# Lead tiles of the FFN opening on normalized quarters: root spreads at fixed places, two lead tiles at a time

## The chip, the cores and the metric

The kernel runs on one core of one Trainium2 chip, in one launch. The metric is the device time of that launch in microseconds; the kernel before was timed three times (median 1522.23), and one further execution was recorded by the hardware profiler. TensorE multiplies matrices, VectorE and ScalarE work on 128-partition tiles, GpSimd does small copies here, and the DMA queues bring the weights in.

## The reference

One inference step of a two-layer decoder trunk with 1024 channels, for 512 prompt positions and 8 sequences of 8 sample positions (576 columns together). Layer 0 has a convolution and windowed attention as its mixer, layer 1 a Mamba-2 mixer; both mixers end in an output projection that is added to the residual `x`, and behind each stands the block that the change touches:

```python
def rmsnorm(x, g):
    xf = x.astype(jnp.float32)
    xf = xf * lax.rsqrt(jnp.mean(xf * xf, axis=-1, keepdims=True) + EPS)
    return xf.astype(x.dtype) * g
...
def conv_ffn(h, hist, w_gate, w_up, conv_w, conv_b, w_down):
    gate = h @ w_gate
    padded = jnp.concatenate([hist, gate], axis=1)
    gc = causal_dwconv(padded, conv_w, conv_b)
    y = (jax.nn.silu(gc) * (h @ w_up)) @ w_down
    return y, padded[:, -(FFN_CONV_WIDTH - 1):]
```

Here `h` is `rmsnorm` of the layer's residual with the norm's gains, `w_gate` and `w_up` have 2816 columns, and the convolution over time has width 3. All values are float32.

## The kernel before

**Products.** Activations lie with channels on the partitions: eight tiles `x0` to `x7` of 128 channels by 576 columns, worked on in two halves of 288 (`HALF`). A float32 product is three TensorE matmuls: each operand is split in a rounded high part and the residual low part, and high times high, high times low and low times high are added up in one PSUM bank (`mm3`, L286, L289, L290). For every tile of weights, ScalarE therefore makes `wh` (L276) and VectorE `wl` (L277), from a buffer `wr` that a DMA fills; `wr`, `wh` and `wl` have three buffers each.

**The norm.** The output projection (`out_proj`, L453) adds its tiles to `x` (`add_x`, L451), the last four for half 0 and then for half 1, and ScalarE and VectorE sum the squares (`sq_add`, L337). When a half is complete, `rstd` (L310) sums over the partitions on TensorE (`pt`, L317), takes the root on ScalarE (L324) and the reciprocal on VectorE (L325 to L329, which end in `dg`), and spreads the result over all partitions by a matmul (`pr`, L333), copied out as `rs` (L335).

**The opening of the FFN.** 22 tiles of gate and of up follow (`ffn`, L475). The first four of gate and two of up are lead tiles: plain products with a pair `h` = g*x, not yet normalized, made by `norm_tile` (high part L411 on ScalarE, low part L412 on VectorE) while the projection still runs. Their results are multiplied by `rs` when they leave PSUM: gate at L521, L524 and L525 on VectorE, up through the gate's SiLU at L510. Behind a gate tile, `gate_done` saves conv history (GpSimd, L497, L498) and computes conv (ScalarE L501, VectorE L503 twice) and SiLU (L506, L507); `gate_open` (L489, L490) begins a gate buffer on GpSimd.

All other tiles go in pairs through a Strassen scheme, seven products in place of eight (`Strassen`, L53 to L150; first product L106, L109, L110). It takes normalized activations in quarters (channels 0 to 511 or 512 to 1023, by half): B11, B12, B21, B22 and the sums T1 to T4. `combine` (L364) makes them between the lead tiles: `hf` = x*g*rs (L373), the differences (L376), and for each piece a high part (ScalarE L361) and a low part (VectorE L362). Its three stages run ahead of gate 3, up 0 and up 1. B12 is not a quarter of its own there. For a Strassen job the sums of weights `st` are made by VectorE (L66, L69 to L71), and their splits at L75 and L76.

**What sets the order.** Each engine runs its instructions in a fixed order that a scheduler derives from the program; an instruction that is marked (`keep_in_program_order`, or `pin=True` in `mm3`) keeps its place among TensorE's. Engines meet through semaphores, and a buffer with a new name waits for the readers of the old one.

## Time and profile before

| | |
|---|---|
| runs | 1522.0, 1522.23, 1522.6 us (median 1522.23) |
| profiled execution | 1524.2 us, of which the span of the instructions is 1522.4 |
| busy, share of the span | TensorE 97%, VectorE 79%, ScalarE 54%, GpSimd 13% |
| mean granted TensorE clock | 0.987 |
| opening of layer 0 | about 214 to 279 us |
| opening of layer 1 | about 1109 to 1173 us |

An opening is counted here from the matmuls `pt` of half 0 to the first product of the second Strassen job. In the profile a row of the timeline has the start, the duration, the engine and line, the operation, and "output <- inputs"; square brackets give idle time before it and what ended it. "PE" is TensorE, "PEld" its weight loads, "DVE" VectorE, "ACT" ScalarE, "POOL" GpSimd and "SPq" a DMA queue. A group row has the number of instructions, the total and mean (ns) duration, and the idle time ahead of them.

### The profile page before, as it was taken

Reading aid. Unit: us, or ns where it says so; the run is one execution under the profiler, and the core shown is the slowest. Engines: PE = TensorE matmul, PEld = TensorE weight load, DVE = VectorE, ACT = ScalarE, POOL = GpSimd, SP = SyncE. Lnnn points to the kernel's source line nnn. Section 1 sums busy time; section 2 is a strip of 40 time slices with the busy share of each in tenths; the row PEclk is TensorE's granted clock in tenths of the full one; section 3 lists DMA queues with packets and bytes.
Section 4 is the critical chain, followed back from the end, with each engine's and each line's share of the span. In section 5 each row is a group of like instructions: output and inputs, shape, how many; then the busy total and the mean of one; then the engine's idle time right before and its main releaser. Section 6 shows DMA issues by size and latency. Waiting matters only on the chain.

```text
span 1522.4 us, 28606 instructions
## 1 busy us (share of the span) xinstructions
PE 1470.3 (97%) x11179; PEld 1398.1 (92%) x11179; DVE 1207.7 (79%) x2283; ACT 827.2 (54%) x1650; POOL 191.2 (13%) x365
## 2 busy tenths in 40 slices
PE   8999997999999999999999999999897999999999
PEld 7968797999999999898988988998897999999998
DVE  7968899977787786778887787777899887877773
ACT  6357466644545443587755754656565554545441
POOL 0035103000000000011312102102002000000000
PEclk9999998999999999999999999999998999999999
DMA  7514221422223322236246245245213322233222
GB/s 225 157 37 115 83 97 29 138 84 84 84 85 99 108 80 64 72 101 208 70 141 196 72 129 178 83 132 167 80 56 97 98 84 84 85 105 99 88 69 84
DMA packets 74551, 157.81 MB, mean 104 GB/s; under 512 B 20383, under 2 KB 25119, under 8 KB 74415
## 3 DMA queue, kind: packets, MB, share of 16 engines
q1 hardware_dynamic: 74414, 155.97, 33.0%
q8 instruction: 88, 1.44, 0.4%
q14 instruction: 49, 0.39, 0.1%
HBM read 140.73 MB, written 15.21 MB: 102 GB/s over the span
## 4 chain that ended last, share of the span: by engine, by line
PE 40%; DVE 6%; ACT 2%; DMA 2%; issue 1%; SPq 0%; ACTq 0%
PE mm L290 8%; PE mm L286 8%; PE mm L289 8%; PE x L106 3%; PE x L109 3%; PE x L110 3%; DMA acb<-acd 2%; PE y L110 1%; PE y L106 1%; PE y L109 1%; DVE wl L277 1%; PE pst L1379 1%; PE z L109 1%; PE z L106 1%; PE z L110 1%; ACT wh L276 1%
## 5 line engine op out<-in xcount | busy, mean ns | idle before, releaser
L290 PE MATMUL mm<-hh,wl 128*128 128x288 f32 x1056 | 318.0, 303 | 22.0 <-DVE wl L277 22.0
L286 PE MATMUL mm<-hh,wh 128*128 128x288 f32 x1056 | 322.1, 306 | 7.4 <-ACT wh L276 5.2
L289 PE MATMUL mm<-hl,wh 128*128 128x288 f32 x1056 | 319.1, 303 | 0.7 <-DVE hl L309 0.4
L290 PEld LDWEIGHTS mm<-hh,wl 128*128 128x128 f32 x1056 | 203.7, 193 | 26.1 <-DVE wl L277 23.2
L286 PEld LDWEIGHTS mm<-hh,wh 128*128 128x128 f32 x1056 | 203.6, 193 | 16.2 <-ACT wh L276 5.6
L289 PEld LDWEIGHTS mm<-hl,wh 128*128 128x128 f32 x1056 | 203.6, 193 | 4.2 <-issue 1.6
L276 ACT ACTIVATE wh<-wr 128x1024 fp32r<-128x1024 f32 (+2 forms) x107 | 108.5, 1014 | 107.0 <-PE mm L289 88.9
L451 DVE TENSOR_TENSOR x<-x,mm 128x288 f32<-128x288 f32 x256 | 113.6, 449 | 51.8 <-PE mm L290 51.5
L277 DVE TENSOR_TENSOR wl<-wr,wh 128x1024 fp32r<-128x1024 f32 (+2 forms) x107 | 127.5, 1194 | 31.7 <-ACT wh L276 31.6
L290 PE MATMUL mm<-yh,vl 128*128 128x288 f32 x512 | 151.2, 295 | 0.0
L286 PE MATMUL mm<-yh,vh 128*128 128x288 f32 x512 | 151.1, 295 | 0.0
L289 PE MATMUL mm<-yl,vh 128*128 128x288 f32 x512 | 151.1, 295 | 0.0
L290 PE MATMUL mm<-yh,wl 128*128 128x288 f32 x448 | 133.9, 300 | 4.3 <-DVE wl L277 4.3
L286 PE MATMUL mm<-yh,wh 128*128 128x288 f32 x448 | 135.2, 303 | 0.0
L289 PE MATMUL mm<-yl,wh 128*128 128x288 f32 x448 | 134.6, 301 | 0.0
L75 ACT ACTIVATE wh<-st 128x512 fp32r<-128x512 f32 x152 | 92.1, 624 | 31.2 <-PE x L109 23.1
L76 DVE TENSOR_TENSOR wl<-st,wh 128x512 fp32r<-128x512 f32 x152 | 103.3, 686 | 2.1 <-ACT wh L75 0.7
L286 PEld LDWEIGHTS mm<-yh,vh 128*128 128x128 f32 x512 | 96.4, 188 | 0.0
L290 PEld LDWEIGHTS mm<-yh,vl 128*128 128x128 f32 x512 | 96.4, 188 | 0.0
L289 PEld LDWEIGHTS mm<-yl,vh 128*128 128x128 f32 x512 | 96.3, 188 | 0.0
L503 DVE SCALAR_TENSOR_TENSOR gconv<-gbuf,par,gconv 128x592 f32<-128x592 f32 x88 | 72.9, 831 | 25.1 <-ACT gconv L501 24.8
L290 PEld LDWEIGHTS mm<-yh,wl 128*128 128x128 f32 x448 | 85.3, 191 | 5.8 <-DVE wl L277 4.5
(395 smaller groups left out, 4001.2 us busy)
## 6 DMA issues: line engine op xcount, KB each, us to landing
wr<-in_w_gate SPq DMA_DIRECT2D x44, 512.0 KB, 3.6
wr<-in_w_up SPq DMA_DIRECT2D x44, 512.0 KB, 4.2
wr<-in_w_in_o SPq DMA_DIRECT2D x40, 512.0 KB, 3.6
wr<-in_w_down SPq DMA_DIRECT2D x64, 256.0 KB, 2.9
h<-in_h SPq DMA_DIRECT2D x32, 256.0 KB, 3.8
acb<-acd SPq DMA_DIRECT2D x32, 256.0 KB, 4.2
out_ssm_s<-h SPq DMA_DIRECT2D x32, 256.0 KB, 2.9
wr<-in_w_out_o SPq DMA_DIRECT2D x16, 512.0 KB, 3.8
```

The lines of the kernel that those rows point to most:

```text
L75: nc.scalar.activation(hi, src, AF.Copy)
L76: nc.vector.tensor_tensor(lo, src, hi.bitcast(F32), op=SUB)
L106: m = nc.tensor.matmul(out, hi[:, ws], xh, start=first and k == 0, stop=False, skip_group_check=skip)
L109: nc.tensor.matmul(out, hi[:, ws], xl, start=False, stop=False, skip_group_check=skip)
L110: nc.tensor.matmul(out, lo[:, ws], xh, start=False, stop=k == 3, skip_group_check=skip)
L276: nc.scalar.activation(hi[:, a:b], raw[:, a:b], AF.Copy)
L277: nc.vector.tensor_tensor(lo[:, a:b], raw[:, a:b], hi[:, a:b].bitcast(F32), op=SUB)
L286: first = nc.tensor.matmul(out, hi[:, ws], xh[:, sl], start=i == 0, stop=False)
L289: nc.tensor.matmul(out, hi[:, ws], xl[:, sl], start=False, stop=False)
L290: nc.tensor.matmul(out, lo[:, ws], xh[:, sl], start=False, stop=i == n - 1)
L451: nc.vector.tensor_tensor(self.x[m][:, sl], self.x[m][:, sl], p[:, :HB], op=ADD)
L503: nc.vector.scalar_tensor_tensor(cv[:, :592], g[:, k:592 + k], w(k), cv[:, :592], op0=MUL, op1=ADD)
```

## The change

The lead tiles take the normalized quarters too, so there is no pair `h`, no L411 or L412, and results leave PSUM by plain copies on ScalarE (gate) or as they did (up); `sl*rs` (L510) is gone. `rstd` is cut in two: `rstd_begin` (to `dg`) and `rstd_end` (spread and copy). At the last tile of the projection, the weights of gate 0 and 1 are loaded ahead of half 0, and gate 2 ahead of half 1; between them the root of half 0 is spread and `scaled(0)` makes B11 and B21, and the projection's last twelve matmuls are marked to keep their place. `lead` takes two gate tiles at a time and goes through the eight quarter pieces, six matmuls each: gates 0 and 1 on half 0, then gates 2 and 3, in whose middle half 1's root is spread and `scaled(1)` makes B12 and B22. Then come T1, gates 0 and 1 on half 1, T2, gates 2 and 3 on half 1, and up 0 and up 1. T3 and T4 are made behind the first Strassen job's `alpha`. B12 is one quarter more, and gate 1's weights are split as two tiles of 512 columns.

```diff
     def norm_begin(self, gname, early, quarters=None):
+        self.gname, self.early, self.ahead = gname, early, quarters
+        self.h = [] if quarters else [self.pair("h") for _ in range(8)]
...
+    def quarter(self, name, make):
+        src = [make(0)]
+        for k in range(4):
+            if k < 3:
+                src.append(make(k + 1))
+            nc.scalar.activation(q[k][:, 0:HB], src[k], AF.Copy)
+            nc.vector.tensor_tensor(q[k][:, HB:T], src[k], q[k][:, 0:HB].bitcast(F32), op=SUB)
+
+    def scaled(self, half):
+        for name, k0 in (("B11", 0), ("B21", 4)) if half == 0 else (("B12", 0), ("B22", 4)):
+            def make(k):
...
+                self.nc.vector.scalar_tensor_tensor(t, self.x[k0 + k][:, sl], self.pv(self.gname, k0 + k), self.rs[:, sl], op0=MUL, op1=MUL)
+                return t
+            self.quarter(name, make)
...
+            lead = norm and self.ahead and m == 7
+            if lead and hf == 0:
+                self.lead = [self.whole(self.ahead[0]), self.halved(self.ahead[1])]
+            if lead and hf == 1:
+                self.lead.append(self.whole(self.ahead[2]))
+                self.rstd_end(self.rs, root, HALF[0])
+                self.scaled(0)
...
+                if lead and hf == 0:
+                    root = self.rstd_begin(self.ssq, self.o1024, HALF[0])
...
-            if f < LEAD_U:
-                nc.vector.tensor_tensor(sl, sl, rs, op=MUL)
...
-                    nc.vector.tensor_tensor(gate_open(f)[:, 2:290], p[:, :HB], rs[:, :HB], op=MUL)
+                    nc.scalar.activation(gate_open(f)[:, 2:290], p[:, :HB], AF.Copy)
...
-                nc.vector.tensor_tensor(g[:, 290:514], p[:, 0:224], rs[:, HB:NP], op=MUL)
-                nc.vector.tensor_tensor(samples(g)[:, :, 2:10], bt(p[:, 224:288]), bt(rs[:, NP:]), op=MUL)
+                nc.scalar.activation(g[:, 290:514], p[:, 0:224], AF.Copy)
+                nc.scalar.activation(samples(g)[:, :, 2:10], bt(p[:, 224:288]), AF.Copy)
...
+        def lead(half, todo, mid=None):
+            names = ("B11", "B21") if half == 0 else ("B12", "B22")
+            banks = [self.pm() for _ in todo]
+            for k in range(8):
+                if mid and k == 4:
+                    mid()
+                t = self.hq[names[k // 4]][k % 4]
+                xh, xl = t[:, 0:HB], t[:, HB:T]
+                for bank, (ws, _) in zip(banks, todo):
+                    out = bank[:, :HB]
+                    hi, lo = [w[:, k % 4 * P:k % 4 * P + P] for w in ws[k // 4]]
+                    m = nc.tensor.matmul(out, hi, xh, start=k == 0, stop=False)
+                    if k in (0, 4):
+                        self.tc.keep_in_program_order(m)
+                    nc.tensor.matmul(out, hi, xl, start=False, stop=False)
+                    nc.tensor.matmul(out, lo, xh, start=False, stop=k == 7)
+            for bank, (_, evac) in zip(banks, todo):
+                evac(half, bank)
...
-        self.units([lead_gate(f) for f in range(3)], 3)
+        g01 = [(w, lead_gate(f)) for f, w in enumerate(self.lead[:2])]
+        lead(0, g01)
+        g23 = [(self.lead[2], lead_gate(2)), (self.whole(d["w_gate"][l, 3]), lead_gate(3))]
+        root = self.rstd_begin(self.ssq, self.o1024, HALF[1])
+        def other():
+            self.rstd_end(self.rs, root, HALF[1])
+            self.free(self.ssq)
+            self.scaled(1)
+        lead(0, g23, other)
         sums = self.combine()
         next(sums)
-        self.units([lead_gate(3)], 1)
+        lead(1, g01)
         next(sums)
-        self.units([lead_up(0)], 1)
-        next(sums)
-        self.units([lead_up(1)], 1)
-        self.free(self.rs, self.h)
+        lead(1, g23[:1])
+        u = [(self.whole(d["w_up"][l, 0]), lead_up(0))]
+        lead(1, g23[1:])
+        lead(0, u)
+        lead(1, u)
+        u = [(self.whole(d["w_up"][l, 1]), lead_up(1))]
+        lead(0, u)
+        lead(1, u)
```

In the engines' orders the change shows at three places. The first is VectorE at the end of layer 0's output projection, around the root of half 0 (`rv` and `dg`; `hl` is the low part of `h`, `wl` a lead tile's residual weights). Before:

```order
L451 TENSOR_TENSOR x4_81<-x4_81,mm_2606 128x288
L451 TENSOR_TENSOR x5_82<-x5_82,mm_2625 128x288
L325 RECIPROCAL rv_2596<-rv_2596 128x72
L412 SCALAR_TENSOR_TENSOR hl_2335<-x4_81,par_72,hh_2334 128x288
L327 TENSOR_SCALAR rv_2596<-rv_2596,rsc_74 128x72
L344 TENSOR_TENSOR ssq_2324<-ssq_2324,sq_2622 128x288
L328 SCALAR_TENSOR_TENSOR rv_2596<-dg_2595,rsc_74,rv_2596 128x72
L412 SCALAR_TENSOR_TENSOR hl_2337<-x5_82,par_72,hh_2336 128x288
L329 TENSOR_TENSOR dg_2595<-rv_2596,rsc_74 128x288
L344 TENSOR_TENSOR ssq_2324<-ssq_2324,sq_2641 128x288
```

and now, where `wl_2633` belongs to gate 2:

```order
L475 TENSOR_TENSOR x4_81<-x4_81,mm_2579 128x288
L475 TENSOR_TENSOR x5_82<-x5_82,mm_2596 128x288
L346 RECIPROCAL rv_2572<-rv_2572 128x72
L371 TENSOR_TENSOR ssq_2324<-ssq_2324,sq_2593 128x288
L348 TENSOR_SCALAR rv_2572<-rv_2572,rsc_74 128x72
L277 TENSOR_TENSOR wl_2633<-wr_2630,wh_2632 128x1024
L349 SCALAR_TENSOR_TENSOR rv_2572<-dg_2571,rsc_74,rv_2572 128x72
L371 TENSOR_TENSOR ssq_2324<-ssq_2324,sq_2610 128x288
L350 TENSOR_TENSOR dg_2571<-rv_2572,rsc_74 128x288
L475 TENSOR_TENSOR x6_83<-x6_83,mm_2613 128x288
L403 SCALAR_TENSOR_TENSOR hf_2643<-x0_77,par_72,rs_2325 128x288
```

The `hl` rows are gone, a `wl` has come between the steps of the root, and the first scaled piece stands two rows behind `dg`.

The second place is VectorE where the second half's scaled pieces begin in layer 0. Before, they were spread between the sums and the evacuations of the gate tiles:

```order
L373 SCALAR_TENSOR_TENSOR hf_2922<-x0_77,par_72,rs_2325 128x288
L373 SCALAR_TENSOR_TENSOR hf_2923<-x1_78,par_72,rs_2325 128x288
L376 TENSOR_TENSOR hf_2922<-hf_2922 128x288
L376 TENSOR_TENSOR hf_2923<-hf_2923 128x288
L373 SCALAR_TENSOR_TENSOR hf_2924<-x2_79,par_72,rs_2325 128x288
L524 TENSOR_TENSOR gbuf_2750<-mm_2812,rs_2325 128x224
L525 TENSOR_TENSOR gbuf_2750<-mm_2812,rs_2325 128x8x8
L376 TENSOR_TENSOR hf_2924<-hf_2924 128x288
```

Now two operations on the first Strassen job's weights (`wr_3181`) stand ahead of them:

```order
L349 SCALAR_TENSOR_TENSOR rv_2775<-dg_2774,rsc_74,rv_2775 128x72
L350 TENSOR_TENSOR dg_2774<-rv_2775,rsc_74 128x288
L66 TENSOR_TENSOR st0_3185<-wr_3181 128x512
L76 TENSOR_TENSOR dl_3191<-wr_3181,dh_3190 128x512
L403 SCALAR_TENSOR_TENSOR hf_2643<-x0_77,par_72,rs_2325 128x288
L403 SCALAR_TENSOR_TENSOR hf_2645<-x1_78,par_72,rs_2325 128x288
L403 SCALAR_TENSOR_TENSOR hf_2649<-x2_79,par_72,rs_2325 128x288
L392 TENSOR_TENSOR hqB12_2811<-hf_2643,hqB12_2811 128x288
```

All eight scaled pieces of the half follow in one run, and no evacuation stands between them.

The third place is VectorE ahead of the weights of up 0 in layer 0. Before, `wl_3072` closed a run of B22's pieces:

```order
L373 SCALAR_TENSOR_TENSOR hf_2928<-x6_83,par_72,rs_2325 128x288
L373 SCALAR_TENSOR_TENSOR hf_2929<-x7_84,par_72,rs_2325 128x288
L362 TENSOR_TENSOR hqB22_3057<-hf_2926,hqB22_3057 128x288
L362 TENSOR_TENSOR hqB22_3058<-hf_2927,hqB22_3058 128x288
L362 TENSOR_TENSOR hqB22_3059<-hf_2928,hqB22_3059 128x288
L362 TENSOR_TENSOR hqB22_3060<-hf_2929,hqB22_3060 128x288
L277 TENSOR_TENSOR wl_3072<-wr_3069,wh_3071 128x1024
```

and now `wl_3022` stands at the end of the sums and of two convolutions:

```order
L535 SCALAR_TENSOR_TENSOR gconv_2945<-gbuf_2755,par_72,gconv_2945 128x592
L392 TENSOR_TENSOR hqT2_2967<-hf_2663,hqT2_2967 128x288
L535 SCALAR_TENSOR_TENSOR gconv_2945<-gbuf_2755,par_72,gconv_2945 128x592
L535 SCALAR_TENSOR_TENSOR gconv_2956<-gbuf_2759,par_72,gconv_2956 128x592
L414 TENSOR_TENSOR hf_2669<-hf_2669,hf_2649 128x288
L535 SCALAR_TENSOR_TENSOR gconv_2956<-gbuf_2759,par_72,gconv_2956 128x592
L392 TENSOR_TENSOR hqT2_2968<-hf_2665,hqT2_2968 128x288
L414 TENSOR_TENSOR hf_2673<-hf_2673,hf_2653 128x288
L277 TENSOR_TENSOR wl_3022<-wr_3019,wh_3021 128x1024
```

Both pieces of T2 that are left, and all of T3 and T4, come behind it.

## The prediction

> **What bounds the kernel now.** I read three views: the page for the whole, TensorE's waits by releaser for where it stops, and the timeline and the table of windows for the places around those stops.

> ```profile
> span 1522.4 us, 28606 instructions
> PE 1470.3 (97%) x11179; PEld 1398.1 (92%) x11179; DVE 1207.7 (79%) x2283; ACT 827.2 (54%) x1650; POOL 191.2 (13%) x365
> PE mm L290 <- DVE wl L277: 26.2, 6, 7.3
> ...
> 252.90 0.61 PE L290 MATMUL mm<-hh,wl 128*128 128x288 f32 x1 [7.31 <-DVE wl L277]
> 265.14 0.40 PE L290 MATMUL mm<-hh,wl 128*128 128x288 f32 x1 [3.46 <-DVE wl L277]
> 1146.75 0.61 PE L290 MATMUL mm<-hh,wl 128*128 128x288 f32 x1 [5.68 <-DVE wl L277]
> 1158.14 0.61 PE L290 MATMUL mm<-hh,wl 128*128 128x288 f32 x1 [3.93 <-DVE wl L277]
> ```

> TensorE is busy 97% of the span, so a change that leaves its products alone can win only where it stands still or runs slowly. The third line (total, times, longest) puts 26.2 us on one cause: a lead tile whose residual weights `wl` VectorE has not made yet. Four of its six waits, 20.4 us, stand in the two FFN openings: the tile of gate 3 or up 0 in layer 0 (252.90, 265.14) and the same two in layer 1.

> ```profile
> 214.65:278.45 63.80, 53.04 (x376) 52.30 (x370) 60.68 (x130) 37.14 (x74) 15.53 (x16) 0.89 0.19 59
> 1109.53:1172.20 62.67, 53.06 (x376) 52.32 (x374) 60.40 (x130) 36.86 (x73) 12.63 (x16) 0.89 0.19 61
> 248.70:258.90 10.20, 6.00 (x25) 6.00 (x26) 9.62 (x24) 6.01 (x15) 7.71 (x2) 0.50 0.17 52
> 265.80:269.20 3.40, 3.40 (x17) 3.40 (x16) 3.40 (x6) 1.25 (x2) 0.00 (x0) 0.50 0.48 154
> 1143.00:1149.80 6.80, 3.05 (x13) 3.05 (x14) 6.80 (x16) 4.29 (x12) 5.59 (x2) 0.50 0.23 77
> 1156.60:1163.50 6.90, 5.36 (x22) 5.36 (x23) 6.23 (x9) 1.61 (x3) 0.00 (x0) 0.51 0.35 103
> ...
> 218.21 0.30 PE L286 MATMUL mm<-hh,wh 128*128 128x288 f32 x1
> 218.35 0.30 PE L289 MATMUL mm<-hl,wh 128*128 128x288 f32 x1
> 253.30 0.44 PE L286 MATMUL mm<-hh,wh 128*128 128x288 f32 x1
> 253.54 0.44 PE L289 MATMUL mm<-hl,wh 128*128 128x288 f32 x1
> 278.96 0.30 PE L106 MATMUL x<-hqB,wh 128*128 128x288 f32 x1
> 1172.81 0.29 PE L106 MATMUL x<-hqB,wh 128*128 128x288 f32 x1
> ```

> The columns of the windows are length, busy time (count) of PE, PE's weight loads, DVE, ACT and POOL, then the granted clock, DMA share and GB/s. The first two windows are the openings, from the first half's sums of squares to just before the second Strassen job's first product (the last two rows). DVE works 60.7 of 63.8 us and 60.4 of 62.7: **in the openings VectorE is the bound**, TensorE has 53 us to do. The four windows below them show the second loss: after each stop the granted clock is 0.50, and matmuls start 0.24 us apart (253.30, 253.54) in place of 0.13 (218.21, 218.35).

> Loss of TensorE, from these rows: stalls 7.5+3.6 us in layer 0 and, with start-to-start slots, 5.8+4.1 and 0.6 of small ones in layer 1, plus about 40 and 34 matmuls at half clock, 0.107 us more each (4.4 and 3.6). Together 15.7+14.1 = 29.8 us. That is the ceiling of the gain: 1492.4.

> **The change part by part.** The products keep their number, so TensorE's work is unchanged. Prices for VectorE:

> ```profile
> 248.44 1.80 DVE L373 SCALAR_TENSOR_TENSOR hf<-x,par,rs 128x288 f32<-128x288 f32 x4
> 250.15 1.55 DVE L362 TENSOR_TENSOR hqB<-hf,hqB 128x288 fp32r<-128x288 f32 x4
> 251.63 1.22 DVE L277 TENSOR_TENSOR wl<-wr,wh 128x1024 fp32r<-128x1024 f32 x1
> 252.76 3.03 DVE L376 TENSOR_TENSOR hf<-hf 128x288 f32<-128x288 f32 x8
> ...
> L412 DVE SCALAR_TENSOR_TENSOR hl<-x,par,hh 128x288 fp32r<-128x288 f32 x16 | 8.0, 508 | 0.3 <-ACT hh L411 0.2
> L521 DVE TENSOR_TENSOR gbuf<-mm,rs 128x288 f32<-128x288 f32 x4 | 1.8, 440 | 0.3 <-PE mm L290 0.3
> L524 DVE TENSOR_TENSOR gbuf<-mm,rs 128x224 f32<-128x224 f32 x4 | 1.5, 386 | 0.1
> L525 DVE TENSOR_TENSOR gbuf<-mm,rs 128x64 f32<-128x64 f32 x4 | 0.9, 215 | 0.0
> L510 DVE TENSOR_TENSOR gsilu<-gsilu,rs 128x576 f32<-128x576 f32 x2 | 1.5, 750 | 0.0
> L503 DVE SCALAR_TENSOR_TENSOR gconv<-gbuf,par,gconv 128x592 f32<-128x592 f32 x8 | 6.6, 827 | 0.0
> ```

> Start to start, four scaled pieces take 1.71 us, 0.43 each; four differences 0.37 each; one `wl` 1.13 (1.22 recorded). So a record is some 0.08 us longer than its slot, and I take each mean less 0.08.

> (1) Unnormalized pair gone: 16 `hl` a layer, but 12 lie before the sums, where TensorE does not wait; 4 x 0.43 = 1.7 us inside the opening. (2) Gate evacuations to ScalarE: 4 x (0.36+0.30+0.13) = 3.2 us. (3) `sl*rs`: 2 x 0.67 = 1.3. (4) One `wl` fewer after the sums, as three lead tiles are loaded ahead: 1.1. VectorE sheds **7.3 us** in each opening. Scaled pieces, splits and differences keep their number.

> ScalarE takes the twelve evacuation copies, which I price from below at nothing and from above at a copy of a whole half:

> ```profile
> 219.47 0.41 ACT L335 ACTIVATE rs<-pr 128x288 f32<-128x288 f32 x1
> 213.67 1.28 ACT L324 ACT_TABLE_LOAD   x1
> 214.40 0.33 PE L317 MATMUL pt<-ssq,o 128*32 128x72 f32 x8
> 1113.85 0.29 PE L286 MATMUL mm<-hh,wh 128*128 128x288 f32 x1
> wr<-in_w_gate SPq DMA_DIRECT2D x44, 512.0 KB, 3.6
> 250.39 7.67 POOL L490 COPY gbuf<-fhist 128x16 f32<-128x16 f32 x1
> ```

> At 0.41 us each that is at most 4.9 us a layer on an engine busy 37 of 64, hidden unless VectorE waits for a square or a high half behind one; I take nothing. If that cover is gone it costs up to 5 us a layer.

> (5) The start. The first sums (214.40) stood nine slots behind the place that is now fixed: in the change 36 products of the projection follow them. The projection ends at 218.21, so the sums end at 218.21 - 36 x 0.1325 = 213.44 against 214.65: 1.2 us earlier in layer 0, and 1113.85 - 36 x 0.1325 - 0.13 = 1108.95 against 1109.53, 0.6, in layer 1.

> (6) New waits. The matmul that spreads the root is pinned 24 products (3.2 us) behind the sums. In layer 0 its `dg` comes after a table load (1.28), a root, a reciprocal, two `add_x` and a `wl` in VectorE's order, by these slots 5.4 us after the sums: TensorE stands 2.2 us, with the last projection tile and all lead products behind it. The first quarter then needs `rs` (0.41), a scaled piece, a copy and a split; I find the first gate pair's first half ending 3.6 us late in layer 0 and 2.0 in layer 1, where `dg` is ahead of that `wl`. The second half's scaled pieces stand on VectorE behind two operations on the first Strassen weights, whose buffer comes free at about 14.5 us after the sums and lands 3.6 later: VectorE idles some 2.1 us there, and as long again for the root. TensorE has 48 products (6.4 us) of gates 2 and 3 as cover until 21.7, and the first split arrives at 20.8. Every microsecond beyond the margin of 0.9 that the transfer is late is late for TensorE too.

> (7) What is late next. From the second half's first scaled piece (19.6) to the `wl` of up 0 VectorE has, in its order, 8 x 0.43 + 26 x 0.37 + 4 x 0.745 + 1.13 = 17.2 us: ready at 36.7, where TensorE comes at 34.8, **a stop of 2.0 us** (1.9 in layer 1). The bound moves on to the second Strassen job: by the same count its weights are there 58.2 us after the sums (56.5), where TensorE comes at 55.7: 2.3 us (2.2).

> (8) GpSimd. The row at 250.39 is a copy of 16 columns that took 7.67 us, begun while VectorE ran splits and differences without pause; two of these gate buffers are now opened inside such a run. If TensorE or ScalarE needs one at once it costs up to that copy, 7.7 us; otherwise nothing. I take 0.2 us a layer, near nothing, since the convolution behind it has several tiles' time. [...]

> **The sum**, by VectorE. Layer 0: -7.3 work, +1.1 idle (4.2 now against 3.1), -1.2 start = -7.4. Layer 1: -7.3, +0.9 (3.2 against 2.3), -0.6 = -7.0. With GpSimd's 0.4: **-14.0 us**. By TensorE, independent of it: new losses 3.6+2.0+2.3 and 2.0+1.9+2.2 = 14.0 in place of 29.8, so -15.8, if no stop takes the clock. I take -14.2. The profiled execution of 1524.2 (span 1522.4) would take 1510.0; it lies 2.0 above the median of 1522.23, so the forecast is **1508.0**.

> **The clock** decides how far the middle can be trusted.

> ```profile
> 761.36 0.40 PE L290 MATMUL mm<-hh,wl 128*128 128x288 f32 x1 [1.62 <-DVE wl L277]
> ...
> 757.20:760.70 3.50, 2.54 (x19) 2.09 (x17) 3.50 (x7) 3.50 (x11) 1.60 (x2) 1.00 0.00 0
> 760.70:764.10 3.40, 2.74 (x20) 2.74 (x21) 3.34 (x6) 2.08 (x6) 0.67 (x1) 1.00 0.44 143
> 142.90:146.30 3.40, 2.43 (x29) 1.74 (x27) 3.40 (x9) 2.01 (x3) 2.36 (x2) 1.00 0.58 98
> 146.30:149.70 3.40, 3.40 (x18) 3.28 (x15) 2.33 (x11) 1.38 (x5) 0.00 (x0) 0.50 0.63 71
> ```

> A stop of 1.62 us left the clock at 1.00, stops of 3.46 and more halved it; but the window at 142.90, with small matmuls and no long stop, was followed by 3.4 us at 0.50. My stops of 2.0 to 2.3 us lie between.

> **Rivals.**
> A, more: the idle time that I give VectorE (4.2 and 3.2 us) fills, because the scheduler's neighbours run out of step with my hand count; half of the new 14 us of loss goes, 1508 - 7 = 1501. For it: TensorE's count already gives more than VectorE's.
> B, the clock: a 2-us stop halves it for 3.4 us, some 25 products x 0.107 = 2.7 us. Only what no later stop swallows counts, so one to three of them, 1511 to 1516. Against it: 761.36. [...]
> C, slower: lead products now follow a quarter piece by piece. If piece k+1 is not begun until piece k is split, one k takes a scaled piece, a copy and a split in turn, 0.51+0.41+0.45 = 1.4 us and hand-overs, say 1.5, where six products need 0.8. Over 32 steps (8 a half, 2 halves, 2 layers) the loss is 22 us: 1530. It decides from a step of about 1.24 us (14.2 / 32 more than 0.8). Against it: VectorE's order shows the next piece scaled ahead of the split, and then a step is 0.43+0.37 = 0.80.
> D, no change: the loss only moves. All sums now come later, and what the lead tiles win the first Strassen jobs wait for: 1520 to 1523. Against it: VectorE really sheds 7.3 us in each opening.

> **How the numbers follow.** Forecast 62% (1503 to 1511), A 13% (1499 to 1503), B 14% (1511 to 1517), D 6%, C 5%. The range 1499 to 1517 holds A, the forecast and B, with 11% outside it and a little at its ends. Faster by over 0.2% (3 us, about what a measurement of this kernel can tell from no change) is A, the forecast and B: 0.89; D gives 0.06; C 0.05.

> **What would show it.** Right: waits of TensorE on a `wl` in the openings down from 20.4 to about 4 us; a wait of some 2 us on `dg` before the spread in layer 0 only; ScalarE about 60% busy there, unnoticed; the second Strassen job's first product at about 271.6 and 1165.6. (6) falls if `hf` of the second half starts after about 20.5 us from the sums; (7) if the stop is at another weight; B shows as a clock of 0.50 behind a stop of 2 us; C as a wait on `hq` before nearly every k; D as new waits inside the first two Strassen jobs. The prediction is wrong above all if ScalarE, with the evacuations, is late for VectorE's splits.

## The result and the profile after

The changed kernel takes 1512.36 us (median of four runs, 1512.18 to 1513.42) against 1522.31: a ratio of 0.9936, 95% interval 0.9919 to 0.9953, or 10.0 us. A second set gave 1509.24 against 1521.36 (0.9919, 0.9905 to 0.9932), 12.1 us. The profiled execution of after took 1512.18, its span is 1510.4 against 1522.4: 12.0 us. The forecast was 1508.0.

The page of the changed kernel and its waits of TensorE (total, times, longest), the rows that concern the openings:

```profile
span 1510.4 us, 28525 instructions
PE 1467.0 (97%) x11179; PEld 1393.9 (92%) x11179; DVE 1190.4 (79%) x2233; ACT 826.4 (55%) x1652; POOL 203.1 (13%) x365
...
PE x L110 <- DVE wl L76: 4.3, 2, 2.2
...
PE mm L583 <- DVE wl L277: 3.2, 2, 1.6
PE pr L360 <- DVE dg L350: 2.4, 3, 2.0
...
PE mm L579 <- ACT hqB L391: 1.5, 1, 1.5
```

The four waits of 20.4 us are replaced by waits for up 0's weights (3.2), for the second Strassen job's (4.3) and for the root and the first quarter (2.4 and 1.5). VectorE has 50 instructions and 17.3 us less to do. The timeline of TensorE shows where the stops stand in each layer:

```profile
218.28 0.40 PE L360 MATMUL pr<-dg,l 128*128 128x288 f32 x1 [2.02 <-DVE dg L350]
249.68 0.40 PE L583 MATMUL mm<-hqB,wl 128*128 128x288 f32 x1 [1.61 <-DVE wl L277]
271.16 0.40 PE L110 MATMUL x<-hqB,wl 128*128 128x288 f32 x1 [2.17 <-DVE wl L76]
1109.54 0.40 PE L579 MATMUL mm<-hqB,wh 128*128 128x288 f32 x1 [1.49 <-ACT hqB L391]
1138.31 0.40 PE L583 MATMUL mm<-hqB,wl 128*128 128x288 f32 x1 [1.57 <-DVE wl L277]
1159.85 0.61 PE L110 MATMUL x<-hqB,wl 128*128 128x288 f32 x1 [2.17 <-DVE wl L76]
```

The windows (columns as in the prediction) show the opening of layer 0, the stretches ahead of and behind each layer's last stop, and the stretch behind the stop at up 0:

```profile
213.00:272.00 59.00, 52.55 (x390) 50.86 (x390) 55.12 (x116) 40.09 (x88) 17.11 (x14) 1.00 0.19 62
249.60:253.00 3.40, 3.32 (x25) 3.33 (x26) 3.40 (x7) 3.40 (x10) 3.40 (x3) 1.00 0.66 207
267.60:271.00 3.40, 1.39 (x11) 1.15 (x9) 3.40 (x5) 1.56 (x3) 3.32 (x2) 1.00 0.20 29
271.00:274.40 3.40, 3.24 (x17) 3.25 (x18) 3.40 (x7) 0.41 (x1) 3.40 (x1) 0.68 0.76 267
1156.40:1159.80 3.40, 1.28 (x10) 1.04 (x8) 3.40 (x6) 1.56 (x3) 3.40 (x2) 0.99 0.17 30
1159.80:1163.20 3.40, 3.35 (x14) 3.35 (x15) 3.40 (x6) 0.48 (x2) 3.40 (x1) 0.51 0.78 275
```

VectorE is still the bound (55.1 of 59.0 us). No half clock follows the stop at up 0, but one follows the stop of 2.17 us in both layers: some 14 matmuls, 0.107 us more each, 1.5 us.

To see the openings apart from the rest I measure, in each trace, from one matmul of the projection (the mark: 460 matmuls ahead of the first Strassen product, before any root) to the third matmul of the second job (the one that waits), and to the third of the fourth job. Fillers (matmuls that nobody reads, added in some kernels below) are not counted.

| | second job, layer 0 / 1 | fourth job, layer 0 / 1 |
|---|---|---|
| before | 81.86 / 80.39 | 104.69 / 103.33 |
| after | 74.31 / 73.12 | 98.25 / 96.94 |
| difference | -7.55 / -7.27 | -6.44 / -6.39 |

So 14.8 us are won up to the second job and 2.0 given back right behind it; 12.8 are left at the fourth job. The rest of the program differs between executions of the same changed kernel: from the fourth job of layer 0 to the mark of layer 1 it took 791.6 and 790.0 us in two profiles of it (790.6 before). The openings of those two agree within 0.1 us. The experiments are therefore read by this measure first.

### The profile page after: what moved, and what is told of

Its sections match the earlier page's. It is cut to its first block, busy times and chain, and to the rows that moved or that the text cites. A ratio compares the mean times of both kernels' runs of the same rounds, so it can differ in the third digit from the quotient of the medians.

```text
span 1510.4 us, 28525 instructions
## 1 busy us (share of the span) xinstructions
PE 1467.0 (97%) x11179; PEld 1393.9 (92%) x11179; DVE 1190.4 (79%) x2233; ACT 826.4 (55%) x1652; POOL 203.1 (13%) x365
## 4 chain that ended last, share of the span: by engine, by line
PE 80%; DVE 10%; ACT 5%; DMA 3%; issue 1%; POOL 0%; SPq 0%; ACTq 0%; DVEq 0%; POOLq 0%
PE mm L304 15%; PE mm L308 14%; PE mm L307 14%; PE x L110 5%; PE x L106 5%; PE x L109 5%; PE y L109 3%; PE y L110 3%; PE y L106 3%; PE z L109 1%; PE z L106 1%; PE z L110 1%; DVE wl L277 1%; DMA acb<-acd 1%; DMA ea<-acd 1%
## 5 line engine op out<-in xcount | busy, mean ns | idle before, releaser
L304 PE MATMUL mm<-hh,wh 128*128 128x288 f32 x864 | 262.0, 304 | 7.1 <-ACT wh L276 5.3
L307 PE MATMUL mm<-hl,wh 128*128 128x288 f32 x864 | 259.3, 301 | 0.6 <-DVE hl L327 0.4
L308 PE MATMUL mm<-hh,wl 128*128 128x288 f32 x864 | 257.9, 299 | 1.6 <-DVE wl L277 1.6
L304 PEld LDWEIGHTS mm<-hh,wh 128*128 128x128 f32 x864 | 164.3, 191 | 15.8 <-ACT wh L276 5.8
L308 PEld LDWEIGHTS mm<-hh,wl 128*128 128x128 f32 x864 | 163.8, 190 | 4.7 <-issue 2.0
L307 PEld LDWEIGHTS mm<-hl,wh 128*128 128x128 f32 x864 | 164.2, 190 | 4.1 <-issue 1.6
L277 DVE TENSOR_TENSOR wl<-wr,wh 128x1024 fp32r<-128x1024 f32 (+2 forms) x105 | 125.4, 1198 | 32.7 <-ACT wh L276 32.4
## 6 DMA issues: line engine op xcount, KB each, us to landing
wr<-in_w_gate SPq DMA_DIRECT2D x44, 512.0 KB, 3.9
wr<-in_w_up SPq DMA_DIRECT2D x44, 512.0 KB, 4.2
wr<-in_w_in_o SPq DMA_DIRECT2D x40, 512.0 KB, 3.5
wr<-in_w_out_o SPq DMA_DIRECT2D x16, 512.0 KB, 3.8
```

What stands on the lines that cost most here:

```text
L277: nc.vector.tensor_tensor(lo[:, a:b], raw[:, a:b], hi[:, a:b].bitcast(F32), op=SUB)
L304: first = nc.tensor.matmul(out, hi[:, ws], xh[:, sl], start=i == 0, stop=False)
L307: nc.tensor.matmul(out, hi[:, ws], xl[:, sl], start=False, stop=False)
L308: nc.tensor.matmul(out, lo[:, ws], xh[:, sl], start=False, stop=i == n - 1)
```

## The experiments

Theory V: VectorE's work ahead of each weight sets the opening. Theory O: the order does (two tiles at a time, fixed roots). A third question is what the stops of some 2 us cost through the clock. Medians, ratios to the kernel before of the same set with 95% intervals, and the two measures. The kernels gate2_pinned, one_tile and t4_later were timed in one set with the change (after_again), the others in three further sets without it, so those are held against both of the change's ratios, 0.9936 and 0.9919:

| run | median | ratio | second job | fourth job |
|---|---|---|---|---|
| after_again | 1509.24 | 0.9919 (0.9905-0.9932) | 74.33 / 73.11 | 98.25 / 96.99 |
| evac_vector | 1515.17 | 0.9948 (0.9930-0.9967) | 77.85 / 76.84 | 100.27 / 99.19 |
| pair_back | 1513.79 | 0.9931 (0.9908-0.9954) | 76.10 / 77.35 | 98.46 / 101.19 |
| one_tile | 1513.20 | 0.9945 (0.9932-0.9959) | 76.58 / 75.20 | 98.99 / 97.54 |
| gate2_pinned | 1510.38 | 0.9933 (0.9920-0.9945) | 74.94 / 73.88 | 98.86 / 96.22 |
| alpha_pinned | 1515.45 | 0.9954 (0.9938-0.9970) | 73.71 / 70.75 | 102.79 / 100.01 |
| t4_later | 1513.25 | 0.9949 (0.9937-0.9962) | 73.78 / 70.65 | 100.74 / 99.04 |
| fill16 | 1509.35 | 0.9913 (0.9889-0.9937) | 76.29 / 73.07 | 98.70 / 95.87 |
| fill_both | 1509.19 | 0.9917 (0.9901-0.9933) | 74.32 / 73.70 | 96.71 / 96.04 |
| six_gates | 1516.23 | 0.9959 (0.9942-0.9975) | | |
| six_early | 1503.12 | 0.9878 (0.9861-0.9894) | | |
| six_early_fill | 1506.88 | 0.9898 (0.9881-0.9915) | | |

**The change again.** The changed kernel once more.

> The changed kernel itself, as the mark for the runs beside it: 1510 to 1514. A stop of TensorE of about 2 us was followed by slow matmuls in some executions and not in others; if the clock falls by chance of where the stop lies, single times of one and the same program spread by some 3 us, and the slow matmuls of this profile stand behind other stops than in the first one. If the stop's length alone decides, they stand at the same places.

Slow matmuls stood at the same two places, 14 and 15 of them, behind stops of 2.17 us. This run alone speaks for the second reading, a stop's length; the other runs decide against it, since in them three stops of 2.31 to 2.35 us (one_tile, pair_back) take no clock and one of 1.76 (alpha_pinned) does. What the traces show of it stands in the last section.

**Copies on VectorE.**

```diff
-                    nc.scalar.activation(gate_open(f)[:, 2:290], p[:, :HB], AF.Copy)
+                    nc.vector.tensor_copy(gate_open(f)[:, 2:290], p[:, :HB])
...
-                nc.scalar.activation(g[:, 290:514], p[:, 0:224], AF.Copy)
+                nc.vector.tensor_copy(g[:, 290:514], p[:, 0:224])
```

> The changed kernel with the gate tiles' results copied out of PSUM by VectorE again (12 plain copies a layer; 3.2 us by the slots of the kernel before) in place of ScalarE. If VectorE is the bound of the opening (theory V), the second Strassen job's residual weights come 3.2 us later in each layer, TensorE's stop there grows by what the stop at up 0 does not take over, and the whole is 6 to 8 us slower than the change: 1518 to 1520. If the gain came from the new order and the fixed roots (theory O), not from VectorE's smaller load, the copies fit in and the time stays within 1511 to 1514.

The second job comes 3.5 and 3.7 us later than in the change, for 3.2 us of copies: theory V, almost one to one. From the first half's sums to that job VectorE is busy 58.0 and 58.3 us, where the change has 54.5 and 54.7, and idle as long as there, so the whole delay is its work. The timeline of TensorE of this run, at up 0 and at the second job of layer 0:

```profile
250.80 0.61 PE L583 MATMUL mm<-hqB,wl 128*128 128x288 f32 x1 [4.58 <-DVE wl L277]
272.87 0.40 PE L110 MATMUL x<-hqB,wl 128*128 128x288 f32 x1 [0.38 <-DVE wl L76]
```

The stop has moved forward: at up 0 it is 4.58 us in place of 1.61, and its slow matmuls (in layer 1, behind 4.62 us, they start 0.24 us apart) fill the later stop, of which 0.38 is left. So no half clock is paid behind the second job, and at the fourth 2.0 and 2.3 us remain. By the ratios the whole is 2 to 4 us slower than the change; the interval overlaps that of the change's first set, and 1515.17 lies between the two expectations. The openings decide here, not the time.

**The unnormalized pair made again.** It is read by nothing.

```diff
+        if self.ahead:
+            g = self.pv(self.gname, m)
+            h, l = self.spare[m % 2]
+            self.nc.scalar.activation(h[:, sl], x, AF.Copy, scale=g)
+            self.nc.vector.scalar_tensor_tensor(l[:, sl], x, g, h[:, sl].bitcast(F32), op0=MUL, op1=SUB)
```

> The changed kernel, making the unnormalized pair h again (16 copies on ScalarE, 16 residuals on VectorE a layer), which nothing reads. The prediction counted only 4 of the 16 residuals, 1.7 us a layer, since 12 lie ahead of the sums where TensorE does not wait. By that term 3 to 5 us slower than the change: 1515.5 to 1517.5. If all sixteen count, 2 x 6.9 = 14 us: 1526. If they all hide, 1512.4.

The second job is 1.8 us later in layer 0 and 4.2 in layer 1. The 1.8 is near the 1.7 of the prediction's four residuals, but the run does not isolate them: the sums of half 0 now stand 23 and 15 matmuls later in TensorE's order, 3.1 and 2.5 us, and from the sums on VectorE is busy only 0.8 and 1.2 us longer. So the run changed the order too, and the term of 1.7 us stays argued; that sums and root come late is part of the delay (the stop ahead of the spread is now 3.31 in layer 0, and 2.90 in layer 1, where there was none). All sixteen (6.9) do not count. At the fourth job only 0.2 us is left in layer 0, since no half clock follows the stop of 2.35 us there (22.4 us from the second job to the fourth, 23.9 in the change), but 4.3 in layer 1. The times, 1508.7 to 1515.7, spread too far to say more.

**One tile at a time.**

```diff
-        lead(0, g01)
+        lead(0, g01[:1])
+        lead(0, g01[1:])
```

> The changed kernel with gates 0 and 1 taken one after the other on half 0, not two at a time. A step of one tile needs TensorE for 0.4 us, VectorE 0.8 us for a piece, so TensorE waits about 0.4 us in each of eight steps, 3.2 us a layer, in the first tile. If pairs are what saves the opening (theory O), 2 x 3 = 6 us slower than the change. Theory V: the stops ahead of up 0 (1.6 us) and the second job (2.2 us) take it over, VectorE's work being the same, and the time stays within 2 us.

TensorE does wait for a piece in nearly every step: in layer 0 the first tile's 24 matmuls start over 6.6 us, where 3.2 would do. The stop at up 0 takes part of that over (0.98 in place of 1.61). But the second job is 2.3 and 2.1 us later. A row of VectorE in layer 0 says why:

```profile
228.24 0.60 DVE L346 RECIPROCAL rv<-rv 128x72 f32<-128x72 f32 x1 [2.95 <-ACT rv L345]
```

TensorE reaches the sums of half 1 some 2 us later, and VectorE, as busy as in the change (54.6 us in each layer), stands 2.95 us for their root, 0.93 and 1.09 in the change; its idle time up to the second job is 6.0 and 4.5 us, 3.9 and 2.4 in the change. So pairs are worth about 2 us a layer, by what they spare VectorE in waiting, which theory V as I had put it, by work alone, does not give. At the fourth job 0.7 and 0.6 us remain, since the stops of 2.33 and 2.31 us ahead of the second job take no clock (22.4 and 22.3 us from it to the fourth job, 23.9 and 23.8 in the change). The median is 4.0 us above the change's in the same set, between the two expectations.

**Gate 2's weights behind the quarters.** The `wl` is pinned on VectorE.

```diff
-                self.lead.append(self.whole(self.ahead[2]))
                 self.rstd_end(self.rs, root, HALF[0])
                 self.scaled(0)
+                self.lead.append(self.whole(self.ahead[2], True))
```

> The changed kernel with the residual weights of gate 2 made behind the first half's quarters on VectorE, not between the steps of the root. In layer 0 the root should reach TensorE 1.1 us earlier (stop ahead of the spread 2.0 -> about 0.9 us). If VectorE is the bound (theory V), TensorE's earlier start is lost again at the stop ahead of up 0, and the second Strassen job's weights come at the same time: the change's time within 1.5 us. If each stop counts for itself, 1 to 2 us faster.

The stop ahead of the spread falls to 1.07 us, as meant, and yet the second job comes 0.6 and 0.8 us later, not earlier: a stop early in the opening costs nothing while VectorE is behind.

**The second job's weights ahead of its sums; the last sum later.** Two ways to take VectorE work from in front of the 2.17-us stop.

```diff
         self.up = up
+        if first:
+            self.alpha()
...
-        nc.vector.tensor_tensor(s1, a21, a22, op=ADD)
+        pin(nc.vector.tensor_tensor(s1, a21, a22, op=ADD))
```

> The changed kernel with the second Strassen job's first residual weights made ahead of its four sums of weights and one split (4 operations of 0.6 us on VectorE). TensorE's stop of 2.17 us ahead of the second job's first product, and the 13 slow matmuls behind it (13 x 0.107 = 1.4 us), should go. Theory V with the clock: 2 x 3.4 = 6 to 7 us faster than the change, 1505.5 to 1506.5. If only the stop goes and what VectorE did not do there is missed at once by the next product, no change: 1512.

```diff
         self.quarter("T3", lambda k: u[k][:, b])
+        yield
...
-                if n == 0:
+                if n < 2:
                     next(sums)
```

> The changed kernel with the last sum, T4 (four differences and four splits on VectorE, 3.0 us), made behind the second Strassen job's first weights. Theory V: the stop of 2.17 us ahead of the second job's first product is gone or below 0.5 us in both layers. If VectorE's backlog ends there, 2 x 2 to 2 x 3.5 us faster than the change (1505 to 1508); if the backlog reaches to the third and fourth job, as when the sums of weights were put behind, the stop comes up there and the time stays within 2 us of the change.

Both remove the stop: the third matmul of the second job starts up to 2.5 us earlier (0.5 and 0.6 in layer 0, where the stop at up 0, 1.76 and 1.86 us, took the clock in both profiles). Both have a longer one later. The timelines of TensorE of the two kernels, layer 0 of each, at the third job:

```profile
283.50 0.61 PE L113 MATMUL x<-hqB,wl 128*128 128x288 f32 x1 [3.81 <-DVE wl L79]
...
283.22 0.61 PE L110 MATMUL x<-hqB,wl 128*128 128x288 f32 x1 [3.00 <-DVE wl L76]
```

With slow matmuls behind it, the fourth job is 2.1 to 4.5 us later than in the change. VectorE's backlog does not end at the second job; work that is put off there falls due one job on. In these two kernels a stop that goes is no gain, since VectorE has no less to do.

**Filling the stops.** Matmuls that nobody reads, in front of the second job, and then also in front of up 0 (the edit shown is that of the second kernel; the first has the 16 alone).

```diff
+                if n == 1:
+                    filler(16, prev.w3[0][:, 0:P], self.hq["B22"][0][:, 0:HB])
                 new.p1()
...
+        filler(14, g23[1][0][1][0][:, 0:P], self.hq["B22"][0][:, 0:HB])
         lead(0, u)
```

> The changed kernel with 16 matmuls that nobody reads (2.1 us) put ahead of the second Strassen job's first product in each layer, where TensorE stands 2.17 us. If the half clock behind that stop comes from the stop, the 13 slow matmuls run at full speed: 2 x 1.4 = 2.8 us faster than the change, 1509.6. If the half clock has another cause, the filling changes nothing (1512.4), or costs what of it does not fit into the stop (up to 2 us).

> The changed kernel with matmuls that nobody reads in the stops ahead of up 0 (14) and ahead of the second Strassen job (16), in both layers. If slow matmuls follow a stop of TensorE of about 2 us by chance, none is left behind these two places, the opening's third job starts 1.1 to 1.5 us earlier in each layer, and the time is 2 to 3 us below the change's, with less spread than the 7 us of the kernel with 16. If the clock falls for another reason, slow matmuls stand there as before.

In the first, no slow matmuls are left behind the second job (22.4 and 22.8 us from it to the fourth, 23.9 and 23.8 in the change), and in layer 1 the fourth job is 1.1 us earlier. In layer 0, however, the stop at up 0 took the clock this time, though it had not in the change, where it was 1.61 us. The timeline and a window of that kernel:

```profile
248.52 0.40 PE L583 MATMUL mm<-hqB,wl 128*128 128x288 f32 x1 [2.03 <-DVE wl L277]
...
249.00:252.40 3.40, 3.40 (x17) 3.40 (x16) 3.40 (x7) 3.40 (x10) 3.40 (x4) 0.50 0.72 233
```

With both places filled, the windows behind them in layer 0 run at full clock,

```profile
248.00:251.40 3.40, 3.40 (x28) 3.34 (x27) 3.40 (x7) 3.40 (x11) 3.40 (x3) 1.00 0.53 165
270.00:273.40 3.40, 3.40 (x27) 3.40 (x27) 3.40 (x7) 0.68 (x2) 0.00 (x0) 1.00 0.73 248
```

and the fourth job comes 1.5 and 0.9 us earlier than in the change, though TensorE does 30 matmuls more a layer. That the half clock goes with the stop is what the traces show (a clock of 0.50 behind it in the change, 1.00 here); the medians (1509.35, 1509.19) cannot tell it from the change's in the second set, 1509.24.

**Less work for VectorE: six plain gate tiles.** In place of the first Strassen gate job, gates 4 and 5 are lead tiles; the second form, whose edit is shown, also asks for the weights of each further lead tile, up 1's included, one tile earlier; the third adds 14 fillers ahead of gate 4.

```diff
-LEAD_G, LEAD_U = 4, 2
+LEAD_G, LEAD_U = 6, 2
...
+        g4 = [(self.whole(d["w_gate"][l, 4]), lead_gate(4))]
         lead(1, g23[1:])
+        g5 = [(self.whole(d["w_gate"][l, 5]), lead_gate(5))]
+        lead(0, g4)
+        lead(1, g4)
...
-        todo = [Gate(LEAD_G), Up(LEAD_U)]
+        todo = [Gate(LEAD_G), Up(LEAD_U), Up(LEAD_U + 2)]
```

> The changed kernel with two more gate tiles taken as plain lead tiles in each layer in place of the first Strassen gate job (LEAD_G 6). TensorE gets 12 products more a layer (1.6 us); VectorE loses the job's sums and splits of weights and its additions (some 8 us) against two residuals (2.3 us), about 5.9 us a layer. Theory V (VectorE's backlog is what the opening lasts): the stop and the slow matmuls ahead of and behind the second job (2.2 + 1.4 us) go and none comes up at the third, net -2 us a layer, 4 us faster than the change (1505 to 1508). If TensorE's work decides by now, 2 x 1.6 = 3.2 us slower.

> As the kernel with six gates, but the weights of each further lead tile are asked for one tile ahead, since there TensorE stood 3.65 us ahead of gate 4 for ScalarE's high half. Theory V: one stop of about 1.6 us ahead of gate 4, as ahead of up 0 in the change, none of over 0.5 us behind it up to the fourth job, and 2 us a layer less than the change in the opening for 1.6 us more products: 4 us faster than the change, a ratio to the kernel before of 0.988 to 0.990. If the stop ahead of gate 4 stays near 4 us, the time of the kernel with six gates or a little less: 0.993 to 0.996.

> The same with 14 matmuls that nobody reads in the stop ahead of gate 4. If a stop there takes the clock, up to 1.5 us a layer faster than the same kernel without them; if it does not, or if there is no stop, equal or up to 2 us a layer slower.

The first missed, by a stop ahead of gate 4 that waits for ScalarE's high half (first row: layer 0, timeline of TensorE). With the weights asked for earlier it is 0.93 and 0.94 us (second and third row, the next kernel), and nothing of over half a microsecond follows in either opening:

```profile
250.07 0.61 PE L579 MATMUL mm<-hqB,wh 128*128 128x288 f32 x1 [3.65 <-ACT wh L276]
...
249.64 0.40 PE L583 MATMUL mm<-hqB,wl 128*128 128x288 f32 x1 [0.93 <-DVE wl L277]
1131.58 0.40 PE L583 MATMUL mm<-hqB,wl 128*128 128x288 f32 x1 [0.94 <-DVE wl L277]
```

1503.12 against 1522.48 is a ratio of 0.9878 (0.9861 to 0.9894), whose interval lies clear of both of the change's: **19.4 us faster than before**, 6 to 9 faster than the change, with 24 matmuls more in the program. How much of that the earlier requests alone would give with four gates is not shown: no run has them so. Fillers ahead of gate 4 make it 3.8 us slower in the median, with intervals that overlap; the stop is then shorter (0.9 us) than what is put into it (14 x 0.1325 = 1.9 us a layer), which accounts for about half of that.

## Why the prediction was right, and where its sum was short

Windows from the first of the sums of half 0 to the second job's third matmul, layers 0 and 1 of the kernel before, then of the change (the third busy time is VectorE's):

```profile
214.65:279.23 64.58, 53.82 (x382) 53.09 (x375) 61.46 (x131) 37.28 (x75) 15.53 (x16) 0.89 0.20 62
1109.46:1173.07 63.61, 54.00 (x386) 53.22 (x380) 61.27 (x131) 36.99 (x74) 12.63 (x16) 0.89 0.20 64
...
212.80:271.16 58.36, 51.91 (x393) 50.21 (x385) 54.48 (x115) 40.29 (x88) 16.27 (x14) 1.00 0.18 57
1102.82:1159.85 57.03, 51.51 (x392) 50.28 (x385) 54.66 (x115) 39.77 (x87) 16.18 (x14) 1.00 0.18 58
```

- **The bound.** That VectorE limits the openings held: work given back to it comes out at the second job one to one (3.2 us as 3.5 and 3.7), and work that only moves later gains nothing. Where the second job came later without more work (one tile at a time), VectorE's idle time had grown by as much.
- **Terms 1 to 5 and the sum by VectorE.** Forecast up to the second job were -7.4 and -7.0, which with 0.4 for GpSimd make the -14.0, taken as -14.2; measured are -7.55 and -7.27. By the windows above VectorE's work fell by 7.0 and 6.6 us (forecast 7.3) and its idle time rose by 0.8 and not at all (forecast 1.1 and 0.9); the sums came 1.3 and 0.7 earlier behind the mark (forecast 1.2 and 0.6). So in layer 0 each term is right within 0.4 us. In layer 1 two terms are 0.7 and 0.9 too large and cancel: that its total fits is luck. Of the single terms of work only the evacuations were set apart by a run. ScalarE's cover for the copies held: no stop of TensorE ends on one.
- **Step 6.** The stop ahead of the spread was 2.0 us in layer 0 (forecast 2.2), and in layer 1 the wait was for the first quarter, 1.5. VectorE idled 0.6 us ahead of the first Strassen weights, not 2.1: the transfer came earlier than I had put it. The second half's scaled pieces still began where forecast: at 232.4, 19.6 us behind the end of the first of the sums (212.8), against 19.6.
- **Step 7.** Stops of 2.0 and 1.9 ahead of up 0 were 1.6 and 1.6; those of 2.3 and 2.2 ahead of the second job were 2.2 and 2.2. The prediction's own figures for the latter, 58.2 less 55.7, make 2.5, not the 2.3 it took, and its stalls and slow matmuls of layer 0 before add up to 15.5, not 15.7; neither moves the forecast by more than 0.2. Its sign at 1165.6 left out what layer 0 gains; the job's third matmul came at 271.16 and 1159.85.
- **What the sum left out.** It ended at the second job, and took "if no stop takes the clock" for granted behind it. The stop there took the clock in both layers, 14 matmuls and 1.5 us each, of which 1.1 and 0.9 stay: that is rival B (14%), not the forecast, and with it 14.8 becomes 12.8. The fillers show it. 1512.36 lies in B's range of 1511 to 1516, and 1509.24 of the second set in the forecast's own, 4.4 and 1.2 us above the 1508.0; the stated range holds the result because it took B in. B's price was wrong too: it counted 25 slow products, 2.7 us, in a stretch of 3.4 us at half clock, where 14 fit. With the 2.0 us that stay, B's mechanism gives 1510; that 1512.36 lies in its range is in part luck.
- **Rivals.** A fell with the stops where they were forecast. C fell: a step takes what was forecast, and behind the first quarter's own 1.5 us in layer 1 the stops on `hq` are three, of 0.28 to 0.36 us. D was wrong for the change, yet right of any further moving of work, as the two kernels that put work off showed.
- **Still open.** Why one set gives 10.0 us and another 12.1, where the profiled openings give 12.8: single times of one program spread by 1 to 9 us. Of the 3.9 us between the two profiles of the change, 2.3 lie ahead of the mark of layer 0, where one has 3.4 us at half clock from 145.95 on and the other none, and 1.7 between the openings, by waits that I did not follow.

## What to carry to other kernels

Where an engine off the matrix unit is the bound of a stage, count its work and its waits up to the last deadline of its backlog, not up to the first; here the stops that went by putting work off came back one job later. Then look for work that another form of the same computation does not need: two plain tiles in place of a Strassen job cost TensorE 1.6 us a layer and freed VectorE of 5.4 (1190.4 to 1179.7 us busy over the two layers). And price a new stop of some 2 us with what followed such stops here, in some cases 14 slow matmuls, 1.5 us, unless a later stop swallows them.

## What the runs showed of the hardware

In the openings of all these traces, stops of TensorE of 2.9 us and more were followed by a stretch at half clock every time (2.90 in pair_back the shortest, 7.31 in the kernel before the longest). Between 1.76 and 2.35 us both happened: 1.76 (alpha_pinned), 1.86 (t4_later), 1.92 (gate2_pinned), 2.03 (fill16), 2.17 (four times, in the two profiles of the change) and 2.31 (pair_back) halved the clock, in layer 0 of the change for 14 matmuls, while 2.31 and 2.33 (one_tile), 2.35 (pair_back) and the stop of 2.02 ahead of the root's spread, in all eleven traces that have it, did not. Of 1.6 and less none did (1.61 and 1.57 at up 0 in the change).

```profile
268.83:272.24 3.41, 1.24 (x10) 1.08 (x9) 3.41 (x6) 1.36 (x3) 3.41 (x1) 1.00 0.49 147
272.24:275.65 3.41, 3.41 (x16) 3.41 (x16) 2.47 (x5) 1.63 (x3) 2.53 (x1) 0.50 0.50 161
...
266.15:269.56 3.41, 2.36 (x18) 2.12 (x17) 3.41 (x6) 1.75 (x4) 0.54 (x2) 1.00 0.01 2
269.56:272.98 3.42, 2.14 (x16) 2.14 (x17) 3.42 (x6) 1.04 (x2) 0.00 (x0) 1.00 0.52 172
272.98:276.39 3.41, 3.41 (x28) 3.41 (x28) 3.19 (x9) 2.15 (x4) 1.15 (x3) 1.00 0.59 192
```

Behind the first the next window is at 0.50, behind the second the clock stays at 1.00. Of the 119 such windows at full clock in and around the openings of the kernel before and of the change (195 to 306 us, 1080 to 1198), the six in which TensorE was busy 1.49 us or less were each followed by one at 0.50, and none of the others, busy 1.84 us or more, was. Of 901 in the same stretches of all traces, the 21 busy 1.50 us or less were each followed by one at 0.50, none with 1.73 us or more was, and of six between 1.55 and 1.65 two were. So in these traces the place of a stop counts beside its length. By my estimate from these numbers a filler helps by the busy time that it adds to the window: 16 matmuls of 0.1325 us are 2.1 us, to the 1.24 of the first window above. Outside the openings these bounds do not hold: behind the window at 142.90 of the kernel before, with small matmuls, the clock halved though 2.43 us were busy.

A GpSimd copy of 16 columns took 7.05 us (267.72 in the change; the median of the 44 such copies is 0.20) while VectorE was busy 6.99 of the 7.05 us, and no stop of TensorE ended on it.
